# Attention probabilities split into two f16 halves and turned by DMA transposes; score corrections on 64 rows a head

## The chip, the cores and the metric

One NeuronCore of a Trainium2 chip runs the whole program. The metric is the device time of one execution in microseconds (us). TensorE (PE) does matmuls and transposes, VectorE (DVE) and ScalarE (ACT) do the elementwise work, GpSimd (POOL) mostly issues weight loads, and SyncE (SP) issues most other DMAs. Each engine runs its own instructions in order and waits on semaphores.

## The reference, cut to what matters

One residual layer over 1024 tokens of width 1024. The RMS-normalised input is projected by one wide matrix; branch A is attention, branch B a gated delta rule, and both are gated, projected and merged. Branch A has three groups of eight heads of 64; a query sees keys at stride 1, 4 or 16, in blocks of 128 queries:

```python
scores = jnp.einsum('brnqhd,brnkhd->brnhqk', qb, kb) * (dh ** -0.5)
scores = jnp.where(valid[:, None], scores, -jnp.inf)
m = jnp.max(scores, axis=-1, keepdims=True)
p = jnp.exp(scores - m)
den = jnp.sum(p, axis=-1, keepdims=True)
o = jnp.einsum('brnhqk,brnkhd->brnqhd', p / den, vb)
lse = (m + jnp.log(den))[..., 0].transpose(0, 1, 2, 4, 3)
```

The outputs of the three groups are then merged head by head with weights from the softmax denominators.

## The kernel before

Every large product is done in f16 with a high and a low half of each operand: high times high, high times low, low times high (`mm3_steps`, lines 182 to 184). The projection is cut into units of 256 columns. A `Feed` object steps through these units, one step ("tick") being three matmuls of 512 columns (or six of 256), and other work calls `feed.tick(n)` to put n ticks of projection between its own matmuls. TensorE's order is therefore exactly the order in which the code is written; the other engines' order is set by a scheduler that goes by priorities and its own estimate of times, and `tc.high_priority()` moves work up.

Attention runs as six sets, one for each group g = 2, 1, 0 and half of the heads (four heads each), while the units of the next set are projected. In each set `att_run` goes through 16 steps: eight query blocks j, and in each two parities `par`, a step working on two heads (u = 0, 1). A step sees nk blocks of 128 keys: nk is 1 in group 2, and in the first block of a run of tokens elsewhere, and 2 otherwise. Over the six sets that is 52 steps with nk = 1 and 44 with nk = 2. A step has three parts, which stand one iteration apart on TensorE:

- `scores(s)`: for each head one matmul of the high half of q with K and one of its low half (L785, L787) into one PSUM bank of the tag S; the mask with the row maximum on VectorE (L794) and the exponential on ScalarE (L798), into the f32 tile P, named `sm`.
- `turn(s)`: 128x128 f32 transposes of P on TensorE into a bank of the tag G (L808), a copy to f16 on ScalarE (`th`, L813), and the rest on VectorE (`tl`, L814, recorded at the helper's line 86).
- `values(s)`: three matmuls for each head and key block (L831, L833, L835) into a bank of the tag O.

After each part `att_run` yields a number of ticks (`pace`, mostly (2, 2, 1), in the last set (2, 1, 1)).

K holds its high half on partitions 0 to 63 and its low half on 64 to 127, for each head. So that one matmul over 128 rows can meet both, the q tiles Qh and Ql hold the same 64 rows twice. The rotated q and k leave `rope_half` in two tiles, pch and pcl, which have one buffer each; `rope_out` copies them in pieces of 32 partitions to the head tiles with DMAs on SP's queue (L624), and then copies rows 0 to 63 of Qh and of Ql to rows 64 to 127 (L627).

The two last sets also combine the three groups (`combine`): small operations on VectorE after loads on SP's queue (L865), and a transpose through a G bank. After the last set the delta-rule branch, the gates and the output projection follow; the change does not touch them.

Of the kernel before, what the change touches and what calls it, by code (L numbers as in the profile page):

```python
# [11 lines left out]
F16 = mybir.dt.float16  # L12
BF16 = mybir.dt.bfloat16
AF = mybir.ActivationFunctionType
ALU = mybir.AluOpType
# [3 lines left out]
S = 1024  # L19
# [58 lines left out]
def hybrid_block(ctx: ExitStack, tc: tile.TileContext, A):  # L78
# [540 lines left out]
    def rope_out(pt, pieces):  # L619

        with tc.high_priority():
            for name, dst, r0, _ in pieces:
                for hd in range(4):
                    nc.sync.dma_start(out=dst[r0:r0 + 32, hd], in_=pt[name[1]][32 * hd:32 * hd + 32, "AB".index(name[0])])  # L624
            for _, dst, r0, twice in pieces:
                if twice and r0:
                    nc.sync.dma_start(out=dst[64:128], in_=dst[0:64])  # L627

    def rope_tiles():
        return {n: rp.tile([128, 2, S], F16, name=f"pc{n}", tag=f"pc{n}", bufs=1) for n in "hl"}  # L630
# [56 lines left out]
            rope_out(pt, pc)  # L687

    def qk_tiles():
        return [ap.tile([128, 4, S], F16, name=n, tag=n, bufs=2) for n in ("Qh", "Ql", "Ks")]  # L690

    def pieces_of(tiles, what):
        Qh, Ql, K = tiles[:3]
        if what == 0:
            return [("Ah", Qh, 0, True), ("Al", Ql, 0, True), ("Bh", Qh, 32, True), ("Bl", Ql, 32, True)]
        return [("Ah", K, 0, False), ("Al", K, 64, False), ("Bh", K, 32, False), ("Bl", K, 96, False)]

    def tok(g, h, k, j):
        if g == 0:
# [53 lines left out]
    def att_run(g, hs, ts, pace):  # L753

        Qh, Ql, K, Vh, Vl = ts
        steps = [(j, par) for j in range(8) for par in range(2)]
        osbs, Ps, ths, pos = {}, {}, {}, {}
        if (g, hs) == sets[-1]:

            room = ap.tile([128, 2048], F32, name="osbs", tag="Ks", bufs=2)  # L760
            new_osb = lambda j: room[:, j % 7 * 264:j % 7 * 264 + 264]
        else:
            new_osb = lambda j: ap.tile([128, 264], F32, name="osb", tag="osb", bufs=4)

        def blocks(j):
            if g == 2:
                return [j]
            first = j == 0 if g == 0 else j % 2 == 0
            return [j] if first else [j - 1, j]

        def scores(s):
            j, par = steps[s]
            kb = blocks(j)
            nk = len(kb)
            mask = amask[:, 256 - 128 * nk:256] if g < 2 else amask[:, 256:384]
            if par == 0:
                osbs[j] = new_osb(j)
            osb = osbs[j]
            psc = bank("S", 2)
            ks = slice(kb[0] * 128, kb[0] * 128 + 128 * nk)  # L780
            qs = slice(j * 128, j * 128 + 128)
            for u in range(2):
                hd = 2 * u + par
                out = psc[:, u * 256:u * 256 + 128 * nk]
                PE.matmul(out, lhsT=Qh[:, hd, qs], rhs=K[:, hd, ks], start=(u == 0), stop=False,  # L785
                          skip_group_check=True)
                PE.matmul(out, lhsT=Ql[:, hd, qs], rhs=K[:, hd, ks], start=False, stop=True,  # L787
                          skip_group_check=True)
            P = ap.tile([128, 2, 256], F32, name="sm", tag="sm", bufs=2)
            Ps[s] = P  # L790
            for u in range(2):
                hd = 2 * u + par
                with tc.high_priority():
                    V.tensor_tensor_reduce(P[:, u, :128 * nk], psc[:, u * 256:u * 256 + 128 * nk], mask,  # L794
                                           -cexp, -NEG, ALU.add, ALU.min, accum_out=osb[:, 256 + hd:257 + hd])
            for u in range(2):
                hd = 2 * u + par
                SC.activation(P[:, u, :128 * nk], P[:, u, :128 * nk], AF.Exp, bias=osb[:, 256 + hd:257 + hd],  # L798
                              scale=-1.0, accum_out=osb[:, 260 + hd:261 + hd])

        def turn(s):
            nk = len(blocks(steps[s][0]))
            P = Ps.pop(s)
            pt = bank("G", 2)
            for u in range(2):
                for i in range(nk):
                    c = (u * nk + i) * 128
                    PE.transpose(pt[:, c:c + 128], P[:, u, i * 128:i * 128 + 128], ident)  # L808
            n = 256 * nk
            th = ap.tile([128, 512], F16, name="th", tag="th", bufs=2)  # L810
            tl = ap.tile([128, 512], F16, name="tl", tag="tl", bufs=2)
            with tc.high_priority():
                SC.copy(th[:, :n], pt[:, :n])  # L813
                TT(tl[:, :n], pt[:, :n], th[:, :n], ALU.subtract)  # L814
            ths[s] = th, tl

        def values(s):
            j, par = steps[s]
            kb = blocks(j)
            nk = len(kb)  # L820
            th, tl = ths.pop(s)
            if par == 0:
                pos[j] = bank("O", 1)
            po = pos[j]
            for u in range(2):
                hd = 2 * u + par
                out = po[:, hd * 64:hd * 64 + 64]
                vs = slice(hd * 64, hd * 64 + 64)
                for i, b in enumerate(kb):
                    c = slice((u * nk + i) * 128, (u * nk + i) * 128 + 128)  # L830
                    PE.matmul(out, lhsT=th[:, c], rhs=Vh[:, b, vs], start=(hd == 0 and i == 0), stop=False,  # L831
                              skip_group_check=True)
                    PE.matmul(out, lhsT=th[:, c], rhs=Vl[:, b, vs], start=False, stop=False,  # L833
                              skip_group_check=True)
                    PE.matmul(out, lhsT=tl[:, c], rhs=Vh[:, b, vs], start=False, stop=(i == nk - 1),  # L835
                              skip_group_check=True)
# [24 lines left out]
    def combine(hs, j, osb):  # L861
        rows = slice(j * 128, j * 128 + 128)
# [1123 lines left out]
```

## Time and profile before

| | |
|---|---|
| time, three runs | 1083.09, 1085.38, 1090.64 us, median 1085.38 |
| the profiled execution | span 1083.1 us; the shortest of the three runs, 1083.09, has the same value, so nothing to speak of lies around the span |
| TensorE | busy 1052.6 us, 97% |
| VectorE | busy 854.9 us, 79% |
| ScalarE | busy 559.6 us, 52% |
| granted TensorE clock | 0.996 on average |
| attention, first score to last value | about 100 to 551 us from the span's start |

The page gives busy time by engine, the chain of work that ended last, and groups of equal instructions. A matmul's recorded duration has the fill of the array in it, and the next one starts before it ends; what a matmul costs TensorE is therefore the distance from its start to the next start in the timeline.

### The profile page before, as it was taken

The page shows a single profiled execution, that of the slowest core. Times are in us where ns is not written, and L with a number is a line of the kernel's source. Part 1 is how long each engine was busy: PE and PEld are TensorE (multiplying, and loading weights), DVE is VectorE, ACT ScalarE, POOL GpSimd, SP SyncE. Part 2 cuts the span into 40 slices and gives each one's busy share as a digit, 9 for nine tenths or more (in the row PEclk, how much of TensorE's full clock was granted, in tenths as well). Part 3 has the DMA queues.
Part 4 walks back from the last instruction along what each step waited for, and adds up shares of the span by engine and source line. Part 5 has one row for each costly group of instructions (what it writes and reads, how often), then busy time and mean ns, then how long its engine had stood idle before and what let it go on. Part 6 is the DMA issues. An engine that isn't in the chain of part 4 may idle for free.

```text
span 1083.1 us, 23724 instructions
## 1 busy us (share of the span) xinstructions
PE 1052.6 (97%) x9426; PEld 641.4 (59%) x9426; DVE 854.9 (79%) x1967; ACT 559.6 (52%) x1272; POOL 66.5 (6%) x115
## 2 busy tenths in 40 slices
PE   6999999999999999999999999999999999999997
PEld 6894595775966855765645544555545554444443
DVE  5697897878879778979965797976588778799934
ACT  6445766667666565557645534244454345333622
POOL 1200000000000000000000000110200000000000
PEclk9999999999999999999999999999999999999999
DMA  8135531632724431741233457785685523753232
GB/s 295 60 98 136 128 109 55 167 99 66 190 79 132 101 126 47 182 117 59 75 122 136 111 130 175 250 247 159 195 269 167 147 99 101 285 185 123 83 120 78
DMA packets 99632, 148.99 MB, mean 138 GB/s; under 512 B 31152, under 2 KB 64432, under 8 KB 98368
## 3 DMA queue, kind: packets, MB, share of 16 engines
q1 hardware_dynamic: 69264, 85.20, 27.3%
q0 software_dynamic: 12320, 44.11, 13.5%
q10 hardware_dynamic: 17936, 18.16, 4.9%
q8 instruction: 74, 1.21, 0.5%
q14 instruction: 38, 0.31, 0.1%
HBM read 91.66 MB, written 36.90 MB: 119 GB/s over the span
## 4 chain that ended last, share of the span: by engine, by line
PE 59%; DVE 26%; DMA 5%; ACT 4%; issue 3%; SPq 2%; ACTq 0%; DVEq 0%
PE ps_mm L182 14%; PE ps_mm L184 14%; PE ps_mm L183 14%; DVE ca L83 4%; DVE wlo L83 2%; DVE X L86 2%; DVE stmp L86 2%; DVE sm L794 2%; DVE rt L86 2%; PE ps_S L182 1%; PE ps_S L184 1%; PE ps_S L183 1%; DVE tl L86 1%; PE ps_G L808 1%; SPq L624 1%
## 5 line engine op out<-in xcount | busy, mean ns | idle before, releaser
L184 PE MATMUL ps_mm<-h_hi,wlo 128*128 128x512 f16 (+1 forms) x552 | 208.6, 378 | 1.2 <-issue 1.2
L183 PE MATMUL ps_mm<-h_lo,whi 128*128 128x512 f16 (+1 forms) x492 | 185.9, 378 | 1.0 <-DVE h_lo L86 1.0
L182 PE MATMUL ps_mm<-h_hi,whi 128*128 128x512 f16 (+1 forms) x492 | 186.0, 378 | 0.9 <-ACT h_hi L434 0.9
L184 PEld LDWEIGHTS <-wlo 128*128 128x128 f16 x788 | 77.5, 98 | 89.5 <-issue 3.4
L182 PEld LDWEIGHTS <-whi 128*128 128x128 f16 x848 | 83.4, 98 | 70.8 <-issue 0.5
L183 PEld LDWEIGHTS <-whi 128*128 128x128 f16 x848 | 83.4, 98 | 69.1 <-issue 2.2
L182 PE MATMUL ps_mm<-whi,h_hi 128*128 128x256 f16 x384 | 105.1, 274 | 0.0
L798 ACT ACTIVATE sm<-sm,osb 128x128 f32<-128x128 f32 (+1 forms) x160 | 69.5, 435 | 68.7 <-DVE osb L794 62.0
L184 PE MATMUL ps_mm<-whi,h_lo 128*128 128x256 f16 x384 | 104.7, 273 | 0.0
L183 PE MATMUL ps_mm<-wlo,h_hi 128*128 128x256 f16 x384 | 104.7, 273 | 0.0
L86 DVE TENSOR_TENSOR tl<-ps_G,th 128x256 f16<-128x256 f32 (+1 forms) x96 | 51.8, 540 | 21.5 <-ACT th L813 21.0
L794 DVE CUSTOM_DVE_ANT_0 sm<-ps_S,amask 128x128 f32<-128x128 f32 (+1 forms) x192 | 59.2, 345 | 8.5 <-PE ps_S L787 8.3
L83 DVE SCALAR_TENSOR_TENSOR wlo<-wstage,whi 128x1024 f16<-128x1024 f32 x50 | 60.8, 1218 | 4.4 <-ACT whi L165 4.1
L83 DVE SCALAR_TENSOR_TENSOR ca<-xc,cw,ca 128x512 f32<-128x512 f32 x72 | 53.7, 746 | 7.1 <-ACT ca L1001 6.3
L165 ACT ACTIVATE whi<-wstage 128x1024 f16<-128x1024 f32 x49 | 51.3, 1051 | 3.0 <-PE ps_O L183 1.4
L83 DVE SCALAR_TENSOR_TENSOR whi<-wstage,whi 128x512 f16<-128x512 f32 x60 | 40.8, 687 | 13.6 <-ACT whi L329 12.9
L808 PE MATMUL ps_G<-cons,sm 128*128 128x128 f32 x280 | 47.5, 275 | 2.1 <-ACT sm L798 1.0
L183 PEld LDWEIGHTS <-h_hi 128*128 128x128 f16 x384 | 45.8, 119 | 1.6
L329 ACT ACTIVATE whi<-wstage 128x512 f16<-128x512 f32 x60 | 37.1, 626 | 18.5 <-DVE wstage L328 13.4
L182 PE MATMUL ps_mm<-h_hi,wlo 128*128 128x512 f16 x120 | 45.6, 380 | 1.0 <-DVE rx L83 1.0
L182 PEld LDWEIGHTS <-h_hi 128*128 128x128 f16 x384 | 45.5, 119 | 1.5
L184 PEld LDWEIGHTS <-h_lo 128*128 128x128 f16 x384 | 45.5, 119 | 1.5
(436 smaller groups left out, 2584.4 us busy)
## 6 DMA issues: line engine op xcount, KB each, us to landing
wstage<-in_w POOLq DMA_DIRECT2D x68, 512.0 KB, 4.8
og<-osb ACTq DMA_DIRECT2D x32, 132.0 KB, 2.2
og<-og SPq DMA_DIRECT2D x32, 132.0 KB, 2.2
gspb<-gst ACTq DMA_DIRECT2D x16, 256.0 KB, 2.3
sga<-gspa SPq DMA_DIRECT2D x8, 512.0 KB, 6.9
wstage<-in_w_up POOLq DMA_DIRECT2D x8, 512.0 KB, 5.1
wos<-in_w_out SPq DMA_DIRECT2D x8, 512.0 KB, 5.4
sgb<-gspb SPq DMA_DIRECT2D x8, 512.0 KB, 5.9
```

The lines of the kernel that those rows point to most:

```text
L83: (eng or V).scalar_tensor_tensor(out, in0, scalar, in1, op0=op0, op1=op1)
L86: (eng or V).tensor_tensor(out, in0, in1, op)
L165: in_turn(SC.activation(hi[:, 4 * c:4 * c + 4], st, AF.Copy, scale=W_SCALE))
L182: PE.matmul(out, lhsT=wh(k), rhs=mh(k), start=first and i == 0, stop=False, skip_group_check=True)
L183: PE.matmul(out, lhsT=wh(k), rhs=ml(k), start=False, stop=False, skip_group_check=True)
L184: last_pe[0] = PE.matmul(out, lhsT=wl(k), rhs=mh(k), start=False, stop=last and i == len(ks) - 1, skip_group_check=True).ins.name
L329: in_turn(SC.activation(t[:, b, 0], self.part[name], AF.Copy, scale=W_SCALE))
L624: nc.sync.dma_start(out=dst[r0:r0 + 32, hd], in_=pt[name[1]][32 * hd:32 * hd + 32, "AB".index(name[0])])
L794: V.tensor_tensor_reduce(P[:, u, :128 * nk], psc[:, u * 256:u * 256 + 128 * nk], mask, -cexp, -NEG, ALU.add, ALU.min, accum_out=osb[:, 256 ...
L798: SC.activation(P[:, u, :128 * nk], P[:, u, :128 * nk], AF.Exp, bias=osb[:, 256 + hd:257 + hd], scale=-1.0, accum_out=osb[:, 260 + hd:261 ...
L808: PE.transpose(pt[:, c:c + 128], P[:, u, i * 128:i * 128 + 128], ident)
```

## The change

The f32 probabilities are no longer turned on TensorE. ScalarE copies P to f16 (`hi`), VectorE takes the rest (`lo`), both into one tile p16 of 128 x 512 or 128 x 1024, and one DMA transpose on SP's queue writes all its 128x128 blocks to a tile tT, from which `values` takes its stationary operands. `values` comes one iteration later, and the yields at the end of a set are arranged anew. In `scores` the two heads of a step have a bank each (tags S and G); the high products still use 128 rows, but the low half of q meets only the high half of K, on 64 rows: the two heads of a step stand on opposite halves of the partitions, in Ql (which now has two slots and is not copied twice) and in Ks (where for two of the four heads the halves are exchanged). The product of the two low halves is left out. `rope_out` sends the pieces of Qh ahead of those of Ql, and the copy of Ql's rows is gone.

```diff
     def pieces_of(tiles, what):
         Qh, Ql, K = tiles[:3]
+        def at(dst, l, r0):
+            def of(hd):
+                if l == "q":
+                    return dst[r0:r0 + 32, hd]
+                if l == "Q":
+                    return dst[64 * (hd // 2) + r0:64 * (hd // 2) + r0 + 32, hd % 2]
+                r = 64 * ((hd // 2) ^ (l == "l")) + r0
+                return dst[r:r + 32, hd]
+            return of
         if what == 0:
-            return [("Ah", Qh, 0, True), ("Al", Ql, 0, True), ("Bh", Qh, 32, True), ("Bl", Ql, 32, True)]
+            return [("Ah", at(Qh, "q", 0), None), ("Bh", at(Qh, "q", 32), Qh), ("Al", at(Ql, "Q", 0), None),
+                    ("Bl", at(Ql, "Q", 32), None)]
...
-            psc = bank("S", 2)
+            psc = [bank(t, 2)[:, :128 * nk] for t in "SG"]
...
             for u in range(2):
                 hd = 2 * u + par
-                out = psc[:, u * 256:u * 256 + 128 * nk]
-                PE.matmul(out, lhsT=Qh[:, hd, qs], rhs=K[:, hd, ks], start=(u == 0), stop=False,
+                PE.matmul(psc[u], lhsT=Qh[:, hd, qs], rhs=K[:, hd, ks], start=True, stop=False,
                           skip_group_check=True)
-                PE.matmul(out, lhsT=Ql[:, hd, qs], rhs=K[:, hd, ks], start=False, stop=True,
+            for u in range(2):
+                r = slice(64 * u, 64 * u + 64)
+                PE.matmul(psc[u], lhsT=Ql[r, par, qs], rhs=K[r, 2 * u + par, ks], start=False, stop=True,
                           skip_group_check=True)
...
         def turn(s):
             nk = len(blocks(steps[s][0]))
             P = Ps.pop(s)
-            pt = bank("G", 2)
-            for u in range(2):
-                for i in range(nk):
-                    c = (u * nk + i) * 128
-                    PE.transpose(pt[:, c:c + 128], P[:, u, i * 128:i * 128 + 128], ident)
             n = 256 * nk
-            th = ap.tile([128, 512], F16, name="th", tag="th", bufs=2)
-            tl = ap.tile([128, 512], F16, name="tl", tag="tl", bufs=2)
+            p16 = ap.tile([128, 1024], F16, name="p16", tag="p16", bufs=2)
+            hi, lo = [p16[:, n * l:n * l + n].rearrange("p (u k) -> p u k", u=2) for l in range(2)]
+            tT = ap.tile([128, 8, 128], F16, name="tT", tag="tT", bufs=3)
             with tc.high_priority():
-                SC.copy(th[:, :n], pt[:, :n])
-                TT(tl[:, :n], pt[:, :n], th[:, :n], ALU.subtract)
-            ths[s] = th, tl
+                SC.copy(hi, P[:, :, :128 * nk])
+                TT(lo, P[:, :, :128 * nk], hi, ALU.subtract)
+                nc.sync.dma_start_transpose(out=tT[:, :4 * nk], in_=p16[:, :2 * n])
+            ths[s] = tT
...
-        for s in range(n + 2):
+        for s in range(n + 3):
             if s < n:
                 scores(s)
                 yield pace[0]
             if 0 <= s - 1 < n:
                 turn(s - 1)
-                yield pace[1] + (s >= n)
-            if 0 <= s - 2 < n:
-                values(s - 2)
-                yield pace[2] + 2 * (s > n)
+            if s - 1 < n + 1:
+                yield pace[1]
+            if 0 <= s - 3 < n:
+                values(s - 3)
+                yield pace[2]
```

On TensorE, at the scores of a step with nk = 2 in the set of group 1, the rows before are these (Ks is K; ps_S is a bank of tag S; the four rows stand there twice, once for each head):

```order
L785 LDWEIGHTS Qh
L785 MATMUL ps_S<-Ks,Qh 128x256
L787 LDWEIGHTS Ql
L787 MATMUL ps_S<-Ks,Ql 128x256
```

and these now, for both heads, with the projection's first rows behind them:

```order
L798 LDWEIGHTS Qh
L798 MATMUL ps_S<-Ks,Qh 128x256
L798 LDWEIGHTS Qh
L798 MATMUL ps_G<-Ks,Qh 128x256
L802 LDWEIGHTS Ql
L802 MATMUL ps_S<-Ks,Ql 128x256
L802 LDWEIGHTS Ql
L802 MATMUL ps_G<-Ks,Ql 128x256
L182 LDWEIGHTS wlo
L182 MATMUL ps_mm<-h_hi,wlo 128x512
```

The two corrections now stand together, with a full-width product ahead of them and a full-width projection behind, and each of the two heads has its own bank.

On TensorE, where a turn stood between two ticks, before:

```order
L184 LDWEIGHTS whi
L184 MATMUL ps_mm<-sum1h,whi 128x512
L808 MATMUL ps_G<-cons,sm 128x128 x2
L182 LDWEIGHTS wlo
L182 MATMUL ps_mm<-sum2h,wlo 128x512
```

Now nothing stands there, and TensorE has no instruction between a step's scores and its values but projection and other steps. What took its place is on SP's queue. There a q unit's pieces of the group 0 projection stood together before (pch, pcl: the rotated q; og: loads of `combine`):

```order
L624 DMA Qh<-pch 32x1024 x4
L624 DMA Ql<-pcl 32x1024 x4
L624 DMA Qh<-pch 32x1024 x4
L624 DMA Ql<-pcl 32x1024 x4
L627 DMA Qh<-Qh 64x4096
L627 DMA Ql<-Ql 64x4096
L624 DMA Ks<-pch 32x1024 x4
```

and such a unit's pieces stand among the transposes now (p_ is a buffer of p16, the number its own):

```order
L624 DMA Qh<-pch 32x1024 x3
L826 DMA_TRANSPOSE tT<-p_4533 128x4x128
L624 DMA Qh<-pch 32x1024 x4
L826 DMA_TRANSPOSE tT<-p_4588 128x4x128
L624 DMA Qh<-pch 32x1024
L624 DMA Ql<-pcl 32x1024 x3
L826 DMA_TRANSPOSE tT<-p_4670 128x8x128
L624 DMA Ql<-pcl 32x1024 x4
L826 DMA_TRANSPOSE tT<-p_4732 128x8x128
L624 DMA Ql<-pcl 32x1024
L627 DMA Qh<-Qh 64x4096
L826 DMA_TRANSPOSE tT<-p_4787 128x4x128
```

So a transpose is issued only when the pieces ahead of it have been, and the pieces of a unit are spread over some five steps.

More of the change, by code (lines that the diff above doesn't have):

```diff
@@ L621, in rope_out @@
         with tc.high_priority():
-            for name, dst, r0, _ in pieces:
+            for name, dst_of, _ in pieces:
                 for hd in range(4):
[L624 to L627, printed above, removed]
+                    nc.sync.dma_start(out=dst_of(hd), in_=pt[name[1]][32 * hd:32 * hd + 32, "AB".index(name[0])])
+            for _, _, twice in pieces:
+                if twice is not None:
+                    nc.sync.dma_start(out=twice[64:128], in_=twice[0:64])
     def rope_tiles():
@@ L820, in values @@
             nk = len(kb)
-            th, tl = ths.pop(s)
+            tT = ths.pop(s)
             if par == 0:
```

15 lines of the change are left out of this document (8 added, 7 removed).

## The prediction

> **What bounds the kernel now.** I read the page's busy times and chain first, then TensorE's timeline around one attention step, its waits from 100 to 560 us, and the windows of the last sets.
>
> ```profile
> span 1083.1 us, 23724 instructions
> PE 1052.6 (97%) x9426; PEld 641.4 (59%) x9426; DVE 854.9 (79%) x1967; ACT 559.6 (52%) x1272; POOL 66.5 (6%) x115
> PE 59%; DVE 26%; DMA 5%; ACT 4%; issue 3%; SPq 2%; ACTq 0%; DVEq 0%
> ...
> PE ps_O L835 <- DVE tl L86: 2.7, 3, 1.3
> PE ps_S L787 <- DMA Ql<-Ql: 2.3, 1, 2.3
> PE ps_G L808 <- ACT sm L798: 1.0, 3, 0.4
> ```
>
> TensorE is busy 97% of the span and hardly waits in the attention sets: its three largest waits there are the last three rows. So a matmul taken out of TensorE's queue shortens the program by its distance to the next start, as long as VectorE, second in the chain with 26%, keeps up. Where it may not:
>
> ```profile
> core 0: us, PE busy (x) PEld busy (x) DVE busy (x) ACT busy (x) POOL busy (x), PEclk, DMA share, GB/s
> 400.00:440.00 40.00, 39.79 (x287) 22.80 (x285) 35.28 (x104) 24.09 (x64) 1.58 (x3) 1.00 0.31 94
> 486.00:555.00 69.00, 66.32 (x534) 40.29 (x532) 66.13 (x235) 48.12 (x135) 2.11 (x4) 1.00 0.26 78
> ```
>
> By the heading row, VectorE (DVE) is busy 35.28 of 40 us (88%) in the last set but one, and 66.13 of 69 (96%) in the last set. There VectorE is as much the bound as TensorE.
>
> **The transposes that go.**
>
> ```profile
> 308.42 0.38 PE L808 MATMUL ps_G<-cons,sm 128*128 128x128 f32 x2
> 308.64 0.38 PE L182 MATMUL ps_mm<-sum2h,wlo 128*128 128x512 f16 x1
> ...
> L808 PE MATMUL ps_G<-cons,sm 128*128 128x128 f32 x280 | 47.5, 275 | 2.1 <-ACT sm L798 1.0 <-DVE tl L86 0.7
> ```
>
> Two transposes stand from 308.42 to 308.64, 0.108 us each by start to start (the recorded 275 ns have the array's fill in them). 280 of them are 30.2 us off TensorE, and its queue has nothing in their place.
>
> **The corrections.** How many they are, then start to start at both widths, and then the only place before where 64-row tiles alternate between the two row halves and two banks, as they will now (the transposes of the delta rule's output):
>
> ```profile
> L787 PE MATMUL ps_S<-Ks,Ql x192: 216/219/314, 102.8 to 541.1; 128*128 128x128 f16 x104, 128*128 128x256 f16 x88
> ...
> 305.38 0.22 PE L785 MATMUL ps_S<-Ks,Qh 128*128 128x128 f16 x1
> 305.44 0.22 PE L787 MATMUL ps_S<-Ks,Ql 128*128 128x128 f16 x1
> ...
> 305.61 0.38 PE L182 MATMUL ps_mm<-sum1h,whi 128*128 128x512 f16 x1
> ...
> 309.93 0.27 PE L785 MATMUL ps_S<-Ks,Qh 128*128 128x256 f16 x1
> 310.04 0.27 PE L787 MATMUL ps_S<-Ks,Ql 128*128 128x256 f16 x1
> ...
> 310.37 0.38 PE L182 MATMUL ps_mm<-sum2h,wlo 128*128 128x512 f16 x1
> ...
> 905.45 0.38 PE L183 MATMUL ps_mm<-sum2l,wlo 128*128 128x512 f16 x1
> 905.66 0.38 PE L184 MATMUL ps_mm<-sum2h,wlo 128*128 128x512 f16 x1
> 905.97 0.27 PE L1740 MATMUL ps_G<-cons,ob 64*128 64x64 f32 x1
> 905.98 0.27 PE L1740 MATMUL ps_S<-cons,ob 64*128 64x64 f32 x1
> ...
> 906.21 0.22 PE L1740 MATMUL ps_G<-cons,ob 64*128 64x64 f32 x1
> 906.21 0.22 PE L1740 MATMUL ps_S<-cons,ob 64*128 64x64 f32 x1
> 906.37 0.39 PE L182 MATMUL ps_mm<-sum2h,wlo 128*128 128x512 f16 x1
> ```
>
> A score matmul costs 0.055 us with 128 keys and 0.109 with 256. The rows from 905.45 on say two things. Pairs on opposite halves do start together (906.21 and 906.21), so a pair streams in the time of one. But going into these tiles and out of them is not free: the 512-column matmul of 905.66 would have had its successor at 905.88 (some 0.215 later, as it follows the one of 905.45), and the first tile starts at 905.97, 0.09 late; the last pair, which streams some 0.06 (its distance from the pair before), is followed at 906.37, 0.10 late. I charge 0.19 us to each step. A step with nk = 1 paid 2 x 0.055 = 0.11 and now pays 0.055 + 0.19, 0.135 more; one with nk = 2 paid 0.218 and now pays 0.109 + 0.19, 0.081 more. 52 and 44 steps: 7.0 + 3.6 = 10.6 us **lost**. The bounds: 7.7 us gained (half of 104 x 0.055 + 88 x 0.109 = 15.3) if the f16 pairs switch for nothing, and 18.2 lost (96 x 0.19) if they don't overlap. I take the rows' own value, because the neighbours are the same full-width f16 matmuls.
>
> [...]
>
> **The first wait.**
>
> ```profile
> 102.77 0.22 PE L787 MATMUL ps_S<-Ks,Ql 128*128 128x128 f16 x1 [2.33 <-DMA Ql<-Ql]
> ```
>
> The copy of Ql's rows is gone, the copy of Qh stays last in its queue, so this wait goes: 2.3 us.
>
> **The DMA transposes and their cover.** No transposing DMA is in this trace. The nearest rows: plain DMAs of the attention sets, the small-piece copies of the delta rule, and what SP needs to issue (4 in 2.44 us).
>
> ```profile
> Qh<-Qh SPq DMA_DIRECT2D x5, 512.0 KB, 4.6
> gspa<-gst SPq DMA_DIRECT2D x4, 256.0 KB, 2.5
> MT<-u_d SPq DMA_DIRECT2D x8, 128.0 KB, 7.5
> 145.00 2.44 SPq L624 DMA_DIRECT2D Ks<-pch  x4
> ```
>
> A step moves 128 KB (nk = 1) or 256 KB (nk = 2). Bounds for 256 KB: 2.5 us, the plain copy, and 15, twice the 7.5 of the 128 KB that go in short pieces. I take 4, near Qh<-Qh, which also goes from SBUF to SBUF. The cover:
>
> ```profile
> 314.00 0.27 PE L785 MATMUL ps_S<-Ks,Qh 128*128 128x256 f16 x1
> ...
> L794 DVE CUSTOM_DVE_ANT_0 sm<-ps_S,amask 128x256 f32<-128x256 f32 x88 | 33.5, 417 | 1.3 <-PE ps_S L787 1.3
> L798 ACT ACTIVATE sm<-sm,osb 128x256 f32<-128x256 f32 x60 | 30.0, 501 | 32.9 <-DVE osb L794 27.6 <-issue 5.4
> L798 ACT ACTIVATION_READ_ACCUMULATOR sm<-sm,osb 128x1 f32 x160 | 30.0, 188 | 0.0
> L86 DVE TENSOR_TENSOR tl<-ps_G,th 128x512 f16<-128x512 f32 x44 | 30.1, 683 | 5.4 <-ACT th L813 5.1
> L813 ACT CAST th<-ps_G 128x512 f16<-128x512 f32 x44 | 24.9, 565 | 1.0 <-PE ps_G L808 0.8
> L1751 ACT ACTIVATE osb<-zb 128x512 f16<-128x512 f32 x8 | 4.9, 627 | 1.4 <-DVE osb L83 0.8 <-DVE zb L83 0.5
> ```
>
> Scores follow each other at 309.93 and 314.00, so a period is 4.07 us here, some 3.72 after the change (less 0.432 for four transposes, plus 0.081). From `scores(s)` to `values(s)` there are now three periods and p0 + p1 ticks of 0.65 us, over 13 us. Against them: mask 0.42, two exponentials 2 x 0.69, hi 0.63 (L1751 reads SBUF, as hi now does), lo 0.68: 3.1 us, and 2 more in the queues of busy engines. So 8 us are left for a transfer of 4. Nearer is the loop through p16's two buffers: hi of step s + 2 waits on ScalarE until the transpose of step s has landed, so hi + lo + transfer must fit in two periods: 7.4 - 1.3 = **6.1 us** at nk = 2. Behind a waiting hi stand ScalarE's weight splits and evictions. Up to there the transposes cost nothing. They are also queued on SP behind rotated pieces at 0.61 us each, up to four at a time, 2.4 us: 4 + 2.4 is at the edge of 6.1, so in the ten q and k units whose pieces mix with transposes I charge 0.2 each, **2 us** in all (bounds 0 and 15, taking 1.5 for each). ScalarE pays 0.06 us more for each hi (627 against the 565 ns of th), 96 x 0.06 = 6 us in all, hidden in its idle time (it is busy 48.12 of 69 us even in the last set); VectorE's work has the same sizes as before.
>
> **The last set.** There TensorE would save 14 x 0.351 + 2 x 0.081 = 5.1 us (0.432 - 0.081 and 0.216 - 0.135 a step), but VectorE has only 69 - 66.13 = 2.9 us of idle time to give. And the set's end has little to cover the last transpose: four ticks, 2.6 us, stand between the last turn and its values, and the old path of two copies is longer by the transfer. I give back 5.1 - 2.9 = 2.2 and 2 for the end: **4.2 us**.
>
> **The sum:** 1083.1 - 30.2 + 10.6 - 2.3 + 2 + 4.2 = 1067.4. The profiled execution is 2.3 us below the median of the runs shown (1085.38), so the forecast for a median is 1069.7, say **1070 us**, 1.4% faster.
>
> **The rivals.**
>
> - *The pairs gain after all.* If the switch is cheap where the 64-row operands are f16 (those of the quoted tiles are f32), the corrections bring 7.7 and not -10.6: 1070 - 18 = 1052 (1045 to 1060). Against it: 0.10 us of the switch lies ahead of a full-width f16 matmul in the quoted rows too.
> - *Given back in queues.* The last set but one has VectorE at 88%; if it gives back its 5.1 us too, and the ten mixed units cost 1 us each more, or if the pairs do not overlap (7.6 more), the time is 1078 to 1085, no change that can be told. For it: pch has one buffer, its pieces now leave over some five steps, and ScalarE's next write to pch waits for them.
> - *Slow transposes: slower.* Place: the loop through p16. Point: at 256 KB, a transfer above 6.1 us stretches the period to (T + 1.3)/2; 13 us are given back once 44 steps lose 0.3 each, at T = 6.7. Price: at the short-piece rows, T = 15 and 7.5, the periods are 8.2 and, with 0.8 for the smaller hi and lo, 4.1, some 0.5 over the mean of today's: 44 x 4.4 + 52 x 0.5 = 220, so 1290; at T = 9 it is 44 x 1.4 = 63, so 1133. For it: every block lands in tT as rows of 256 bytes, 128 f16 values. Against it: both ends are SBUF, and the short-piece rows go through DRAM in a stretch with busier DMA engines.
>
> [...]
>
> **How the numbers follow.** Chances: the forecast (1060 to 1074) 0.42, the pairs gain 0.15, given back (1074 to 1096) 0.25, slow transposes 0.18. The likeliest is the forecast. The range leaves out the slow transposes and the lowest tail: 1045 to 1095. About 1% is what a measurement of this kernel can tell from no change, so faster means below 1074.5: 0.42 + 0.15, less a little for the edge, 0.55; within 1% 0.23; slower 0.22.
>
> **What the profile after would show.** L808 gone and projection in its place; each pair of L802 starting together, about 0.19 us more around it than its stream; no wait for Ql at the first scores; the transposes landing in about 4 us, TensorE's waits at the values under 10 us in all; VectorE near full in the last set. I am wrong if the values wait for tT step after step, if ScalarE's hi waits for a landing, or if the pairs stand one behind the other.

## The result, and the profile after

The changed kernel takes 1118.73 us (median of 4 runs, 1118.13 to 1119.53), the kernel before 1084.24 (4 runs): ratio 1.0311, 95% interval 1.0269 to 1.0353. It is **3.1% slower**; the forecast was 1070, the range 1045 to 1095. The page's head and chain, and TensorE's and SP's waits of the changed kernel:

```profile
span 1117.8 us, 23465 instructions
PE 1047.3 (94%) x9146; PEld 604.6 (54%) x9146; DVE 855.6 (77%) x1967; ACT 568.5 (51%) x1272; POOL 66.5 (6%) x115
PE 69%; DVE 12%; DMA 7%; ACT 6%; issue 3%; SPq 2%; DVEq 0%; ACTq 0%
```

```profile
PE ps_G L907 <- DVE osb L86: 14.1, 1, 14.1
PE ps_O L843 <- DMA tT<-p: 13.3, 7, 5.5
PE ps_O L843 <- ACT osb L852: 7.6, 6, 2.0
PE ps_G L907 <- DVE osbs L86: 7.3, 3, 3.7
SPq L826 <- DVE p L86: 161.9, 58, 9.3
```

TensorE is busy 5.3 us less than before and idle 40.0 us more (1117.8 - 1047.3 against 1083.1 - 1052.6): that is the 34.7 us of the span. The waits name four lines: the merge's transposes (L907) wait for VectorE, the values (L843) for a transpose or for the eviction of the O bank (L852) on ScalarE. The last row is SP: 58 times a transpose (L826) stands at the head of its queue and waits for VectorE's lo, the tile the trace calls p. This sum is not a loss by itself (in e4 below, a faster kernel with the pieces elsewhere, it is 263.3 us): it costs something only where a transfer that is ready stands behind. What SP pays to issue, and how long to landing:

```profile
L826 SPq DMA_TRANSPOSE tT<-p x96: 1188/1232/3136, 104.4 to 582.7; - x96
DMA to landing us min/median/max: 2.4/3.1/9.8
...
L624 SPq DMA_DIRECT2D Ql<-pcl x48: 507/588/1784, 72.8 to 471.8; - x48
```

A transpose costs SP 1.23 us, twice a piece. Typical landings (issue to landing) are quicker than the 4 us that I took; the tail is not: eight of the 96 took longer than the 6.1 us that the prediction had as the limit of the loop through p16.

One stretch, 460 to 492 us, in order of time. First SP's own rows, then VectorE's, then the chain (start, length, what) that ends in the longest wait:

```profile
460.96 1.26 SPq L826 DMA_TRANSPOSE tT<-p  x1
462.27 3.90 SPq L624 DMA_DIRECT2D Ql<-pcl  x6
466.28 1.25 SPq L826 DMA_TRANSPOSE tT<-p  x1
469.81 2.52 SPq L624 DMA_DIRECT2D Ql<-pcl  x2
```

```profile
470.52 0.69 DVE L86 TENSOR_TENSOR p<-sm,p 128x512 f16<-128x512 f32 x1 [2.81 <-ACT p L824]
475.78 1.23 DVE L86 TENSOR_TENSOR pcl<-rt,pch 128x1024 f16<-128x1024 f32 x1 [4.57 <-DMA Ql<-pcl]
```

```profile
462.27 9.54 DMA Ql<-pcl
471.82 3.84 DMA Ql<-pcl
475.78 1.23 DVE pcl L86
...
481.69 0.60 DVE p L86
...
486.08 1.13 DVE wlo L83
...
491.72 0.34 DVE osb L86
492.11 0.69 PE ps_G L907 x2
```

The eight pieces of Ql leave SP over ten microseconds, between transposes, and they are slow to land as well: the chain begins with a landing of 9.54 us, of a piece issued at 462.27, and one of 3.84. The DMA engines were full then (mean busy share 1.06 from 460 to 476, where 1 is all 16 engines busy; the trace's packet times can add up to more): two transposes (8.83 and 7.51 us to landing) and two 512 KB weight loads from GpSimd's queue (issued at 459.76 and 462.08) were under way with the pieces. VectorE, in order, waits 2.81 us for a hi and then 4.57 for the last piece out of the single pcl buffer. From 475.78 it works with hardly a break through what has piled up; the merge's operations come last, and TensorE, which met their transpose at 478, stands 14.1 us.

And the clock. Windows of the first set, around TensorE's wait of 5.55 us for a transpose, which ended at 130.08 (the column PEclk is the granted clock):

```profile
core 0: us, PE busy (x) PEld busy (x) DVE busy (x) ACT busy (x) POOL busy (x), PEclk, DMA share, GB/s
126.00:130.00 4.00, 0.00 (x0) 0.00 (x0) 0.00 (x0) 0.00 (x0) 0.00 (x0) 0.59 1.14 120
130.00:132.00 2.00, 1.92 (x11) 0.90 (x11) 1.45 (x7) 1.31 (x3) 0.00 (x0) 0.50 0.00 0
132.00:134.00 2.00, 2.00 (x9) 0.81 (x9) 2.00 (x4) 1.69 (x7) 0.00 (x0) 0.62 0.47 98
134.00:136.00 2.00, 2.00 (x19) 1.00 (x17) 2.00 (x7) 1.56 (x4) 0.00 (x0) 1.00 0.61 166
```

The granted clock falls to a half during the wait (0.50 from 127 on) and stays there for some 3 us afterwards, until about 133.5. The transpose that ended the wait was slow to land, not only late to leave:

```profile
120.25 9.79 DMA tT<-p
130.08 0.23 PE ps_O L843
```

Here too the DMA engines were full (DMA share 1.14 from 126 to 130), with two weight loads issued at 118.05 and 120.55. Over the whole execution the granted clock is 0.977, against 0.996 before.

Where the time went, from the first scores of a set to the first of the next (last row: to the first score of the last step), us, read from the timelines of one profiled execution each; the last three columns are experiments told of below:

| set | before | after | layout, PE turns (e17) | pieces on GpSimd (e4) | last sets on PE, three p16 (e13) |
|---|---|---|---|---|---|
| 1 | 66.1 | 74.0 | 62.7 | 64.2 | 61.4 |
| 2 | 67.1 | 68.5 | 68.1 | 69.2 | 67.8 |
| 3 | 72.0 | 79.5 | 78.0 | 72.7 | 74.2 |
| 4 | 71.9 | 73.1 | 74.0 | 72.3 | 73.3 |
| 5 | 107.7 | 121.7 | 107.2 | 115.1 | 111.9 |
| 6 | 55.8 | 63.1 | 55.2 | 61.9 | 57.3 |

### The profile page after: what moved, and what is told of

Its sections match the earlier page's. It is cut to its first block, busy times and chain, and to the rows that moved or that the text cites. A ratio compares the mean times of both kernels' runs of the same rounds, so it can differ in the third digit from the quotient of the medians.

```text
span 1117.8 us, 23465 instructions
## 1 busy us (share of the span) xinstructions
PE 1047.3 (94%) x9146; PEld 604.6 (54%) x9146; DVE 855.6 (77%) x1967; ACT 568.5 (51%) x1272; POOL 66.5 (6%) x115
## 3 DMA queue, kind: packets, MB, share of 16 engines
q0 software_dynamic: 12320, 44.11, 13.3%
## 4 chain that ended last, share of the span: by engine, by line
PE 69%; DVE 12%; DMA 7%; ACT 6%; issue 3%; SPq 2%; DVEq 0%; ACTq 0%
PE ps_mm L182 17%; PE ps_mm L183 16%; PE ps_mm L184 16%; DMA tT<-p 3%; ACT sm L813 2%; DVE rt L86 2%; DMA Ql<-pcl 2%; PE ps_S L182 2%; PE ps_S L184 2%; PE ps_S L183 2%; SPq L624 2%; DVE p L86 1%; DVE sm L809 1%; DMA og<-og 1%; ACT rx L599 1%
## 5 line engine op out<-in xcount | busy, mean ns | idle before, releaser
L182 PE MATMUL ps_mm<-h_hi,whi 128*128 128x512 f16 (+1 forms) x492 | 188.9, 384 | 0.9 <-ACT h_hi L434 0.9
L183 PE MATMUL ps_mm<-h_lo,whi 128*128 128x512 f16 (+1 forms) x492 | 188.3, 383 | 1.0 <-DVE h_lo L86 1.0
L183 PEld LDWEIGHTS <-whi 128*128 128x128 f16 x848 | 83.6, 99 | 78.8 <-issue 8.1
L86 DVE TENSOR_TENSOR p<-sm,p 128x256 f16<-128x256 f32 (+1 forms) x96 | 52.1, 543 | 34.9 <-ACT p L824 34.5
L824 ACT CAST p<-sm 128x256 f16<-128x256 f32 (+1 forms) x96 | 48.0, 500 | 17.6 <-DMA tT<-p 15.9
L843 PE MATMUL ps_O<-Vh,tT 128*128 128x64 f16 x280 | 36.1, 197 | 21.5 <-DMA tT<-p 13.3
L809 DVE CUSTOM_DVE_ANT_0 sm<-ps_S,amask 128x128 f32<-128x128 f32 (+1 forms) x96 | 33.2, 345 | 17.3 <-PE ps_G L802 17.0
```

Source lines behind the costliest of these rows:

```text
L86: (eng or V).tensor_tensor(out, in0, in1, op)
L182: PE.matmul(out, lhsT=wh(k), rhs=mh(k), start=first and i == 0, stop=False, skip_group_check=True)
L183: PE.matmul(out, lhsT=wh(k), rhs=ml(k), start=False, stop=False, skip_group_check=True)
L809: V.tensor_tensor_reduce(P[:, u, :128 * nk], psc[u], mask, -cexp, -NEG, ALU.add, ALU.min, accum_out=osb[:, 256 + hd:257 + hd])
L824: SC.copy(hi, P[:, :, :128 * nk])
L843: PE.matmul(out, lhsT=th, rhs=Vh[:, b, vs], start=(hd == 0 and i == 0), stop=False, skip_group_check=True)
```

## The experiments

Theory: the transposes share SP's one in-order queue with the pieces and the merge's loads; what is late there holds VectorE and ScalarE through single buffers, and they hold TensorE. Rivals: the switch of the 64-row pairs; the transfers themselves; the loop through p16; VectorE as the bound. Differences between kernels are taken from their ratios to before (one hundredth is 10.8 us), as each group of experiments had its own runs of before.

**Corrections and layout.** e1: only the corrections and what they need, on the kernel before.

```diff
-                PE.matmul(out, lhsT=Ql[:, hd, qs], rhs=K[:, hd, ks], start=False, stop=True,
+                PE.matmul(psc[u], lhsT=Ql[r, par, qs], rhs=K[r, 2 * u + par, ks], start=False, stop=True,
```

> The kernel before with the score corrections on 64 rows a head (and the pieces of q and k laid out for it), the f32 transposes still on TensorE. Its two score tiles take both S banks. Theory (the switch into and out of 64-row tiles is a fixed 0.19 to 0.20 us a step): 10.6 us more for the corrections, less the 2.3 of the first wait: 1084.2 + 8.3 = 1092.5 us. Rival (the pairs are worth their halved stream, and the loss lies in the transposes alone): 7.7 + 2.3 less, 1074. Rival (the pairs are a large part of the 34.5 us lost): 1105 or more.

1095.3 us, ratio 1.0113 (1.0086 to 1.0141): 12 us more. e17 takes the same kernel and gives each correction all 128 rows:

```diff
-                PE.matmul(psc[u], lhsT=Ql[r, par, qs], rhs=K[r, 2 * u + par, ks], start=False, stop=True,
+                PE.matmul(psc[u], lhsT=Ql[:, par, qs], rhs=K[:, 2 * u + par, ks], start=False, stop=True,
```

> The first experiment's kernel (transposes on TensorE, the new layout and order of the pieces), with each correction over all 128 rows instead of 64. Theory (a step loses 0.19 us to the switch and gains half its correction stream): 10.6 us less than with pairs, 1095.3 - 10.6 = 1084.7, that is the kernel before within 2 us. Rival (the layout and the order of the pieces cost the 12 us): 1092 to 1096. Rival (the doubled rows of Ql were a cost): 1079 to 1082.

1090.65 us, 1.0067 (1.0045 to 1.0089). TensorE's rows of one step with nk = 1, first e1, then e17:

```profile
199.42 0.28 PE L798 MATMUL ps_S<-Ks,Qh 128*128 128x128 f16 x2
199.63 0.23 PE L802 MATMUL ps_S<-Ks,Ql 64*128 64x128 f16 x2
199.79 0.39 PE L182 MATMUL ps_mm<-sum5h,whi 128*128 128x512 f16 x1
```

```profile
206.02 0.28 PE L798 MATMUL ps_S<-Ks,Qh 128*128 128x128 f16 x2
206.13 0.28 PE L801 MATMUL ps_S<-Ks,Ql 128*128 128x128 f16 x2
206.25 0.27 PE L182 MATMUL ps_mm<-whi,h_hi 128*128 128x256 f16 x1
```

0.37 us against 0.23: the pair loses 0.14 (I had 0.135), about 0.10 going in and 0.10 going out. TensorE's busy time is 1062.5 us in e1 and 1051.1 in e17, 11.4 apart; I had 10.6. In time only 5 us of it appear, and the intervals touch, because e17 waits more. So the rest, 7 us, is not the switch but what else e17 changes: the **layout and the order of the pieces**, and that the scores of a step now take both S banks. No run separates these. At one place in the third set, e1:

```profile
285.11 1.23 DVE L86 TENSOR_TENSOR pcl<-rt,pch 128x1024 f16<-128x1024 f32 x1 [4.78 <-DMA Ql<-pcl]
```

With all pieces of Qh ahead of those of Ql, pcl is read last, and VectorE's next write to it waits; TensorE then waits 2.66 us there for the scores' bank in e1 and 4.43 in e17 (where the trace puts VectorE's wait, 5.24 us, down to another DMA, og<-osb). Neither kernel has a DMA transpose, and in e1 SP sends the pieces without a break; the last one, issued at 275.30, still takes 9.59 us to land, with two weight loads issued at 271.32 and 273.66 beside it. The set takes 78.8 and 78.0 us in place of 72.0.

e2 makes e17's edit in the changed kernel:

> The changed kernel, but each correction runs over all 128 rows of Ql and Ks instead of 64; the low half of k then also meets the low half of the other head's q, terms of the size that the change leaves out. DMAs, banks and the order of everything else stay. Theory (the switch costs 0.19 us a step where TensorE is the bound, and the waits are another matter): TensorE is 18.2 us quicker by 96 x 0.19, slower by 7.7 for the doubled stream, so 10.6 less where nothing waits; I expect 4 to 10 less, 1109 to 1115. Rival (TensorE is bound by waits all through the attention sets, so the switch is hidden): 1117 to 1120. Rival (the pairs gain): 1126.

1114.04 us, 1.0282 (1.0225 to 1.0338): 3 us less, overlapping intervals. TensorE's busy time falls by 13.2 us, its idle time grows by 6.6; where TensorE waits, the switch is mostly hidden. e9 sends the pieces of the changed kernel in the old order:

```diff
-            return [("Ah", at(Qh, "q", 0), None), ("Bh", at(Qh, "q", 32), Qh), ("Al", at(Ql, "Q", 0), None),
+            return [("Ah", at(Qh, "q", 0), None), ("Al", at(Ql, "Q", 0), None), ("Bh", at(Qh, "q", 32), Qh),
```

> The changed kernel with the pieces of q sent in the order of before (first the pieces of both halves' A part, then of B), so that pcl is not read last. Theory (the transposes between the pieces are what is late, the order adds to it): VectorE's wait of pcl for Ql<-pcl falls from 9.2 to some 3 us and the time by 2 to 8: 1110 to 1117. Rival (the order of the pieces is the main loss): 1095 to 1105. Rival (no part in it): 1117 to 1120.

1113.85 us, 1.0274 (1.0228 to 1.0320). The wait of pcl for Ql<-pcl falls from 9.2 to 2.3 us, as expected; the 4 us in time are within the intervals.

**The queue.** e4 moves the pieces off SP:

```diff
-                    nc.sync.dma_start(out=dst_of(hd), ...
+                    nc.gpsimd.dma_start(out=dst_of(hd), ...
-                    nc.sync.dma_start(out=twice[64:128], in_=twice[0:64])
+                    nc.gpsimd.dma_start(out=twice[64:128], in_=twice[0:64])
```

> The changed kernel with the pieces of q and k (and the copy of Qh's rows) issued from GpSimd's queue, which else only carries the weight loads; the transposes stay on SP with the loads of the merge. Theory (one in-order queue on SP): as for the transposes on ScalarE, 1080 to 1100. Rival (the transfers themselves are slow or crowd the DMA engines): 1112 to 1125. Rival (the pieces now stand behind weight loads that wait for their buffers, the same coupling on another queue): over 1120, with long waits for the first scores of a set.

1098.58 us, 1.0154 (1.0104 to 1.0203): **17 us less** than the changed kernel, at the upper end of what the theory said. Its busy times, then two of TensorE's waits:

```profile
PE 1037.1 (95%) x9146; PEld 600.7 (55%) x9146; DVE 856.2 (78%) x1967; ACT 568.4 (52%) x1272; POOL 164.4 (15%) x313
```

```profile
PE ps_O L843 <- DMA tT<-p: 9.1, 7, 3.6
...
PE ps_G L907 <- DVE osb L86: 2.0, 1, 2.0
```

The wait of 14.1 us at L907 is now 2.0, VectorE's wait for Ql<-pcl is gone from its list, the granted clock is 0.991. The transposes' landings are no quicker (median 3.9 us; 27 of the 96 took over 5 us, against 17 in the changed kernel), so quicker transposes are not what gave the 17 us. Nor does e4 show emptier DMA engines: at the place of the 5.55 us wait the same two weight loads run in e4 (issued at 118.28 and 120.78), and the window from 120 to 128 is this, first of the changed kernel, then of e4:

```profile
120.00:128.00 8.00, 4.53 (x29) 1.97 (x27) 2.82 (x9) 2.22 (x8) 0.53 (x1) 0.92 1.14 193
```

```profile
120.00:128.00 8.00, 7.26 (x50) 3.45 (x48) 6.39 (x18) 4.86 (x16) 5.05 (x11) 1.00 1.01 241
```

The engines are full in both (share 1.14 and 1.01), but TensorE is busy 4.53 us of the eight in the one and 7.26 in the other. Over 100 to 600 us the DMA share is 0.59 in the changed kernel and 0.60 in e4. e18 makes the same edit in the kernel before:

> The kernel before, with only the pieces of q and k (and the copies of Qh's and Ql's rows) issued from GpSimd's queue. Theory (SP's queue is late only because the transposes stand in it): no gain without them, 1082 to 1088. Rival (the pieces are better off on GpSimd's queue in any case): 1065 to 1075.

1090.68 us, 1.0066 (1.0042 to 1.0091): 7 us **more**. The other queue is no gain by itself; what e4 relieved is that pieces and transposes share one. e3 moves the transposes instead:

```diff
-                nc.sync.dma_start_transpose(out=tT[:, :4 * nk], in_=p16[:, :2 * n])
+                nc.scalar.dma_start_transpose(out=tT[:, :4 * nk], in_=p16[:, :2 * n])
```

> The changed kernel with the transposes issued from ScalarE's queue instead of SP's, where the pieces of q and k and the loads of the merge stay. Theory (one in-order queue: the transposes wait on SP for VectorE's lo, the pieces and loads behind them leave late, and the transposes behind pieces leave late; VectorE and ScalarE are then held by the single buffers): the waits for tT, for Ql<-pcl and for og fall to a third, TensorE's 40 us of added idle time by half or more and its clock comes back: 1080 to 1098, although ScalarE pays 96 x 1.2 us for the issues. Rival (the transfers themselves are slow or crowd the DMA engines): 1112 to 1125, with the same landing times. Rival (ScalarE is held at each issue until lo is done): over 1120.

1147.72 us, 1.0595 (1.0567 to 1.0623): the time of the last rival, but mostly not by its mechanism. Pieces and tT are on time (pcl waits 1.8 us for Ql<-pcl, TensorE 1.4 us for tT). What holds ScalarE is the issuing itself: the 96 issues take 135 us of its queue, and its waits just ahead of them, for lo or anything else, add up to some 21. The theory had counted the issues (96 x 1.2 us) and taken them as affordable; what stands behind them on ScalarE, the eviction of the O bank above all, is late:

```profile
L826 ACTq DMA_TRANSPOSE tT<-p x96: 1204/1249/2893, 105.3 to 613.1; - x96
```

```profile
PE ps_O L843 <- ACT osb L852: 25.6, 13, 3.5
```

**Buffers, traffic, VectorE.** e6, a third p16 in the changed kernel:

```diff
-            p16 = ap.tile([128, 1024], F16, name="p16", tag="p16", bufs=2)
+            p16 = ap.tile([128, 1024], F16, name="p16", tag="p16", bufs=3)
```

> The changed kernel with a third buffer for p16, so that hi of a step no longer waits for the transpose two steps earlier; all transposes and pieces stay on SP's queue. Theory (SP's in-order queue is what is late; p16 only passes it on): ScalarE's 15.9 us of waits for tT go, but lo, the pieces and the loads behind the transposes stay late: 1108 to 1116. Rival (the loop through p16 itself is the loss): 1085 to 1098. Rival (nothing comes of it): 1117 to 1120.

1110.05 us, 1.0221 (1.0171 to 1.0270), 10 us less, the intervals just touching. ScalarE's waits for a transpose fall from 15.9 to 4.1 us, and TensorE's longest wait at L907 stays (11.6 us). The gain is a little over half of what moving the pieces gave: p16 passes lateness on, as the theory said. e10 turns only hi, e11 also leaves out lo (neither has the low half of the probabilities in its values):

```diff
-                nc.sync.dma_start_transpose(out=tT[:, :4 * nk], in_=p16[:, :2 * n])
+                nc.sync.dma_start_transpose(out=tT[:, :2 * nk], in_=p16[:, :n])
-                TT(lo, P[:, :, :128 * nk], hi, ALU.subtract)      # (e11)
```

> The changed kernel with only the high half of the probabilities turned by DMA: lo is computed but not turned, and the third product of the values takes the high half again. VectorE, ScalarE and TensorE do the same work; half the bytes and packets of the transposes are gone, and a transpose no longer has to wait for lo. Theory (SP's queue is late because transposes wait there for VectorE's lo and take 1.2 us each; the traffic itself matters less): the transposes leave one VectorE operation earlier and the waits fall by a half: 1090 to 1105. Rival (traffic and landing times are the main loss): under 1090. Rival (neither): 1112 to 1120.

> As the kernel with only the high half turned, and lo is not computed at all, so that VectorE has 96 operations of 0.42 and 0.68 us less, some 52 us. Theory (from VectorE's 88 to 96% in the two last sets nothing can be gained there whatever TensorE saves, and in the others it has the room): 10 to 20 less than with lo computed, nearly all of it in the last two sets. Rival (VectorE is not a bound): within 5 of it. Rival (VectorE bounds all six sets): 30 to 50 less.

e10 1106.24 us, 1.0210 (1.0171 to 1.0249); e11 1092.75, 1.0081 (1.0051 to 1.0111). Half the bytes, and no wait for lo on SP, bring 11 us; taking 42 us off VectorE (813.6 against 855.6) another 14, of which the last two sets hold 9.8 (117.8 + 60.3 against 113.5 + 54.8) and the four others together nothing. VectorE is a bound in the last two, as the theory said. Whether e10's 11 us come from fewer bytes or from the earlier issue isn't separated. Even so e11 is not below the kernel before.

**Together.** e5 joins e2's and e4's edits; e7 adds to e5 ticks at the ends of the sets, e8 adds to e5 a third p16 and the merge's loads on GpSimd's queue.

```diff
-                yield pace[1]                      # (e7)
+                yield pace[1] + (s > n)
+            else:
+                yield 3
-            nc.sync.dma_start(out=og[:, i], in_=dram[g, hs][rows])   # (e8)
+            nc.gpsimd.dma_start(out=og[:, i], in_=dram[g, hs][rows])
```

> Both edits together: corrections over all 128 rows, and the pieces of q and k on GpSimd's queue; the transposes stay on SP. Theory (two separate losses, the switch and the queue, each beside the drained set ends): with the waits mostly gone the switch should now show nearer its full 10.6 us: 1098.6 - 8 to -10.6 = 1088 to 1091. Rival (the switch is cheaper than 0.1 us a step and the earlier 5 us were chance): 1095 to 1099. Rival (both edits free the same idle time): 1098.

> As the kernel with both edits, and four more ticks of projection at the end of each set (one ahead of the last but one values, three ahead of the last), where TensorE waits 2 to 3 us a set for the eviction of the O bank and for the last transpose. Theory (the end of a set has nothing left to cover eviction and transpose, 6 x 2.5 us): 6 to 12 below the kernel with both edits. Rival (the ticks are only taken from the next set, which then waits): within 3 of it.

> As the kernel with both edits, and a third buffer for p16 and the loads of the merge on GpSimd's queue too, so that SP carries hardly more than transposes in the attention sets. Theory (what is left of the waits in the merge's sets is the loads behind transposes on SP): VectorE's wait for og falls from 14 us to under 5 and the time by 2 to 6 against the kernel with both edits. Rival (GpSimd's queue delays the loads behind weight loads): no gain, or some us more.

1101.01 us (1.0141, 1.0086 to 1.0196), 1097.76 (1.0122, 1.0066 to 1.0177) and 1102.83 (1.0189, 1.0115 to 1.0263). None differs from e4 by more than the intervals, and the gains that the theories forecast did not come. TensorE's busy time in e5 is 8.7 us under e4's and comes back as waits for the O bank (14.5 us in place of 7.8). In e8 VectorE's wait for the merge's loads falls to 6.8 us, but a wait of 14.8 at L907's place is back; the chain into it goes over VectorE from a store (oa_d<-osb, 7.48 us to landing), not over the merge's loads. e12 turns on TensorE in the two last sets (`if g == 0:` the transposes, copies and lags of the kernel before), the rest as e5.

> The kernel with corrections over 128 rows and the pieces on GpSimd's queue, in which the two last sets (group 0, the ones with the merge) turn their probabilities on TensorE again, with the values one iteration earlier, while the four other sets keep the DMA transposes. Theory (in the last sets VectorE is the bound, the removed matmuls bring nothing, and the later values and merge cost time): the two sets come back to the 108 and 56 us of before from 115 and 59, so 1101 - 10 = 1091. Rival (the two sets are slow for the other edits, or the pieces on GpSimd): 1099 to 1110, since TensorE has 12 us more to do there.

1094.62 us, 1.0099 (1.0068 to 1.0131). The two sets take 112.2 and 57.3 us, where e5 had 114.7 and 59.1: a part of the gain expected, and the intervals overlap. e13 to e16 build on e12: a third p16 (e13); the values of the first four sets in two banks (e14); both (e15); both and ticks at the ends (e16).

```diff
-                pos[j] = bank("O", 1)
+                pos[j] = bank("O", 1) if g == 0 else bank("G", 2)    # (e14 to e16; scores in one S bank)
```

> The kernel with corrections over 128 rows, pieces on GpSimd's queue and the two last sets on TensorE, with a third buffer for p16. Theory (hi waits for the transpose two steps back, and the eviction of the O bank stands behind it on ScalarE): ScalarE's 11 us of waits for tT go, half of TensorE's 15.7 us of waits for the O bank too: 1094.6 - 4 to -8 = 1087 to 1091. Rival (the eviction is late for another reason): 1093 to 1096.

> The same kernel with two buffers of p16, but the values of the four first sets go alternately to the two G banks (the two heads' scores share one S bank, as in the kernel before), so that values no longer wait for the eviction of the block before. Theory (the single O bank is how late ScalarE work reaches TensorE): its 15.7 us of waits fall below 3, and the time by 8 to 13: 1082 to 1087. Rival (the wait only moves to tT, which is late by the same amount): 1091 to 1096.

> Both: a third buffer of p16 and two banks for the values in the first four sets. Theory (both hold one chain, from the landing of a transpose over hi and the eviction to TensorE): 1078 to 1084, at or just below the kernel before. Rival (the transposes land too late for the values anyhow, DMA-bound): 1088 to 1096.

> As before it, with four more ticks at the ends of the four first sets. Theory (what is left are 2 to 3 us a set of waits for the last transpose, which the ticks cover): 4 to 8 less, 1072 to 1078. Rival (ticks taken from the next set): within 2 of it.

| | us | ratio to before | 95% interval |
|---|---|---|---|
| e13 | 1089.72 | 1.0058 | 1.0036 to 1.0080 |
| e14 | 1097.14 | 1.0113 | 1.0063 to 1.0163 |
| e15 | 1092.43 | 1.0085 | 1.0041 to 1.0128 |
| e16 | 1089.19 | 1.0045 | 1.0021 to 1.0070 |

The third p16 does what was expected: ScalarE's waits for tT are gone from e13's list and TensorE's for the O bank fall from 15.7 to 9.0 us, though the intervals of e12 and e13 overlap. e14, e15 and e16 miss what their theories forecast. One row of e14 says why the second bank is no help, beside the row of e12 that it answers:

```profile
PE ps_G L856 <- DMA tT<-p: 18.5, 10, 3.4
```

```profile
PE ps_O L855 <- ACT osb L864: 15.7, 15, 2.0
```

The wait for the eviction became a wait for tT, as its rival said. No kernel with DMA transposes came below the kernel before. The nearest by its interval is e16, 0.2 to 0.7% above it, and no version beats it.

## Why the prediction was wrong, point by point

- **What TensorE saves: right.** Four steps of the third set, before and after, first scores to first scores:

```profile
237.96 0.27 PE L785 MATMUL ps_S<-Ks,Qh 128*128 128x256 f16 x1
...
254.59 0.27 PE L785 MATMUL ps_S<-Ks,Qh 128*128 128x256 f16 x1
```

```profile
251.64 0.27 PE L798 MATMUL ps_S<-Ks,Qh 128*128 128x256 f16 x1
...
267.48 0.27 PE L798 MATMUL ps_S<-Ks,Qh 128*128 128x256 f16 x1
```

  16.63 and 15.84 us: 0.79 less, where the terms for transposes and pairs gave 0.86 for two steps of each nk. By this the whole is 18 us, not 19.6 (30.2 - 10.6). That a matmul is recorded longer than its distance to the next start shows in the rows of the kernel before, by some 0.16 us at each width (0.38 us beside 0.215, 0.27 beside 0.109, 0.22 beside 0.055); that this is the array's fill was my reading, which no run tests.
- **The pairs: right in size** (0.14 a step, 11.4 us of TensorE's time), and the switch of 0.10 each way held with f16 operands (e1's rows above). What the pairs save, 0.055 us a step with nk = 1 and 0.109 with nk = 2, does not pay for it.
- **The first wait, 2.3 us: gone, as forecast, but the sum had no term for its price.** The kernel with the layout and order that took it away (and with both S banks in each step) costs 7 us in e17. I looked at the start of the first set and not at who writes pcl next.
- **The DMA transposes and their cover: the step that failed.** The landing of 4 us was near (median 3.1), the 13 us from scores to values too. The failed sentence is the one that charges 0.2 us in each of ten units, 2 us in all, with 15 as the bound. Taking the pieces off the queue gives 17 back, and a third p16, in the changed kernel, 10; no run joins just these two. The sum counted how long pieces delay a transpose. It did not count the other direction, which only the second rival touched: a transpose at the head of SP's queue waits for lo, takes 1.23 us to issue, and shares the queue with pieces and loads that single buffers turn into waits of VectorE, which the prediction itself had at 88 to 96%. Nor did it count crowding: it took one landing time, 4 us, and against the 6.1 of the loop through p16 the trace has eight landings of 6.4 to 9.8 us, while the DMA engines' share was 0.8 to 1.1. The sign that I had named came: hi waits for landings (15.9 us), and the values wait 20.9 us (13.3 for tT, 7.6 for the O bank), not under 10.
- **The last set, 4.2 us given back: the place was right, the size not.** Set 6 lost 7.3 us and set 5 lost 14.0 where TensorE should have saved 5.1 in each. With TensorE turning again and the queue relieved (e13) set 5 still takes 4.2 and set 6 1.5 more than before.
- **The clock: no term at all.** By the step rows TensorE's busy time should have fallen by about 18 us; it fell by 5.3. The other 13 are the lower clock: summed over TensorE's busy stretches, each with the granted clock of the trace, it took 15.9 us in the changed kernel and 3.4 before, 12.5 more.
- **The rivals.** "Given back in queues" named the right mechanism and was far too small. "Slow transposes" was the one on the right side of zero, but its price came from transfers that are slow at every step; the trace has ScalarE's hi waiting 15.9 us for landings, far from the 63 to 220 us of that rival's price. The transposes land in 3.1 us at the median (3.3 those of eight blocks, 2.8 those of four), the merge's plain loads of 132 KB in 2.6. The longest landing, 9.8 us, was of four blocks, in the crowd at 120.25.

What stays open: e13's TensorE is busy 1038.2 us, 14.4 less than before, and its median is 0.6% longer; the runs show the waits moving between O bank, tT and the merge, and no single one that carries the rest. Why sharing the queue costs so much is shown only in part: whether the pieces were late by SP's order of issue or by the transfers ahead of them in the same queue wasn't separated. In both stretches shown in the changed kernel, what was under way on SP's and GpSimd's queues landed late and nearly together, so crowded DMA engines may have a part in the longest waits, which no run tests alone; e4, with as full engines at the first of these places and more landings over 5 us, still won 17 us, so they are not the whole.

## What to carry to other kernels

Work taken off the busiest engine is worth its time only if the engines behind it have slack in every stretch: here VectorE stood at 88 to 96% in the last sets before and, in order, passed late buffers on to TensorE (4.57 us of waiting for a piece, then TensorE's 14.1). Before putting a DMA that waits for late data on a queue, list what stands behind it there, which buffers those transfers release, and who writes them next; after the change, look at the waits for those transfers and those writers, not at the queue's own wait, which rose to 263.3 us in the faster e4. If the queue is that of an engine with work of its own, count the issues too (135 us on ScalarE in e3). Undo the parts singly and together: pieces, buffers, order and switch gave back 17, 10, 4 and 3 us alone (the last two within the noise), but three of them in one kernel (e8, with the merge's loads moved as well) only 13.

## What the hardware showed that I had not expected

At the median a transposing DMA took 1.23 us to issue on SP (the changed kernel) and 1.25 on ScalarE (e3), against 0.59 for a plain piece on SP and 0.50 on GpSimd (e4). Two waits of TensorE in the changed kernel cost more than their length: after 5.55 us of idleness that ended at 130.08 the granted clock was one half until about 133.5 (0.50, then 0.62 in the window from 132 to 134), and after the 14.1 us that ended at 492.11 it was 0.50 until 495. Not every wait brought this: after one of 2.17 us that ended at 427.69 the clock was 1.00. The sum had no price for this. Landings had a long tail: with two weight loads under way a piece of Ql took 9.59 us in e1 and a transpose of four blocks 9.79 in the changed kernel, where the medians are 5.1 and 2.8.
